# Weights stationary and both token tiles moving in the feed forward products, from the fourth chunk on

## The chip, the cores and the metric

The kernel runs on one core of a Trainium2 chip. The metric is the device time of one execution in microseconds, measured over several runs. Its input is one sequence of 256 tokens with 1,024 features, all in fp32, and the weights of three transformer layers, which lie in HBM.

## The reference

Three layers are computed one after the other on `x` of shape 256 x 1024. The first layer is a feed forward, a hybrid mixer (sparse attention and a gated recurrence) and a feed forward, with RMS norms ahead of each. The second and third layers have a feed forward, a mixer (forgetting attention, then latent attention "MLA"), a feed forward and a gate, each followed by a layer norm. The change is in the six feed forwards:

```python
def swiglu(x, w_gu, w_down):                    # layer 1, twice: D_FF = 2752
    gate, up = jnp.split(x @ w_gu, 2, axis=-1)
    return (jax.nn.silu(gate) * up) @ w_down
h = h + 0.5 * swiglu(rms_norm(h, ffn1_norm[l]), ffn1_w_gu[l], ffn1_w_down[l])
...
def swiglu_2(x, w_in, w_out):                   # layers 2 and 3, four times: D_FF_2 = 2816
    h = x @ w_in
    gate, up = h[..., :D_FF_2], h[..., D_FF_2:]
    return (jax.nn.silu(gate) * up) @ w_out
x = post_norm(x, 0.5 * swiglu_2(x, ffn1_w_in[i], ffn1_w_out[i]), ln_g[i, 0], ln_b[i, 0])
```

## The kernel before

The 256 tokens are two tiles of 128, `T` = 0 and 1. For each tile a Python generator (`net`) writes out the whole network, and `run` takes turns between the two: a step takes one unit of weights, and tile 1 follows `lag_at` units behind tile 0 (5, 3, 5 and 4 units in the feed forwards f1, f2, g1 and g2). The order that results is a static one; a scheduler may exchange instructions that wait for something, and gives priority to those written under `urgent`.

Every large product is done in three, since operands are split into a high and a low part (`mm3`, L348 to L350: high x high, high x low, low x high). They are of the type fp32r. The activations lie transposed in tiles `xh` and `xl` (a row block of 128 features by 128 tokens is the stationary operand), and the weights move, up to 512 columns at a time.

Weights come in units (`plan`, `ffn_units`), 512 KB for most, by SyncE's DMA queue into `wr` tiles of 128 x 512 (L312). ScalarE copies each to a high part (L319) and VectorE subtracts to get the low part (L320); both parts are `w` tiles, 42 in all, each 2,048 bytes wide. `AHEAD` = 2 units are written ahead of the one in use.

A feed forward (`ffn`, L580) goes through the hidden units in chunks of 256 (11 chunks; the last has 192 or 256). `up(c)` multiplies x by the gate and up columns of a chunk, 24 products of 512 columns for a token tile (eight row blocks times three), into one PSUM bank. ScalarE takes the tanh (L592) and VectorE forms silu(gate) x up (L593, L595 or L597). One unit into the next chunk's products, `turn` transposes the 128 x 256 result by two TensorE transposes (L358) into bank `tr`, and `split` (L353, L354) gives `hT` in two parts. `down(c-1)` then multiplies `hT` (stationary) by the down weights, 12 products of 512 columns for a chunk and token tile, into the two banks `a`, which collect over all chunks. `done` adds them to x (L572).

A token tile has four PSUM banks: `mm`, `tr` and twice `a`. Behind an RMS norm (f1, f2) the products take x without its factor 1/rms; the factor is a scalar per token, which is a partition there, and comes in by the tanh's scale and at L597.

In the MLA layer `mla_kv` (L1197) has another form: for token tile 0 it computes the keys of both tiles, with the weights stationary and 256 token columns of the tiles `ckh` and `ckl` moving:

```python
nc.tensor.matmul(o, wh[:, hs], xh, start=k == 0, stop=False)    # L1211
nc.tensor.matmul(o, wh[:, hs], xl, start=False, stop=False)     # L1212
nc.tensor.matmul(o, wl[:, hs], xh, start=False, stop=k == 1)    # L1213
```

Other products that the prediction uses: L870 (gated recurrence, plain fp32, 64 columns moving), L1294 (MLA values, plain fp32, 128 columns), L779 (compressed blocks, plain fp32, 256 columns; plain fp32 runs each product as two passes, each of them a record), and L1121 (forgetting gate, fp32r; the stationary operand is one column repeated 128 times, `fsel[:, h:h+1].to_broadcast([P, P])`).

Tiles are laid out in SBUF by `places`: `w`, `xh`, `xl`, `s2`, `wr`, `keep` and others, one behind the other, all with widths that are multiples of 512 bytes.

Of the kernel before, what the change touches and what calls it, by code (L numbers as in the profile page):

```python
# [12 lines left out]
FR = mybir.dt.float32r  # L13
U8 = mybir.dt.uint8
AF = mybir.ActivationFunctionType
# [12 lines left out]
LEVELS = [2, 4, 8, 16, 32, 64]  # L28

AHEAD = 2  # L30
N_WR = 6
N_S2 = 20
N_WARM = 6
N_W = 42
N_SE = 8
HP = 100
HALF = 512
# [17 lines left out]
L_M1 = 5  # L55


def ffn_units(tag, wg, wd, F, extra=()):
    nch = -(-F // 256)

    def up(c):
        f0 = 256 * c
        fw = min(256, F - f0)
        cols = [(f0, f0 + fw), (F + f0, F + f0 + fw)]
        return [(tag + "u", "s", [(wg, P * k, P * k + P, cols) for k in (2 * j, 2 * j + 1)])
                for j in range(4)]

    def down(c):
        f0 = 256 * c
        fw = min(256, F - f0)  # L70
        return [(tag + "d", "s", [(wd, f0 + r, min(f0 + r + P, F), [(0, D)])])
                for r in range(0, fw, P)]

    out = up(0)
    for c in range(1, nch):
        out += up(c) + (list(extra) if c == 3 else []) + down(c - 1)
    return out + down(nch - 1)


def col_units(tag, w, cols, K, per):  # L80
# [184 lines left out]
class Net:  # L265
    def __init__(self, nc, tc, sb, ps, a, units, offs):
        self.nc, self.tc, self.sb, self.ps, self.a = nc, tc, sb, ps, a
        self.units, self.offs = units, offs
        self.c = {}
        self.nw = 0  # L270
        self.live = deque()
        self.sh = {}
        self.uid = 0


# [81 lines left out]
        n = src.shape[0]  # L357
        self.nc.tensor.transpose(out, src, self.c["ident"][0:n, 0:n])  # L358

    def xt_tiles(self, n=8):  # L360
        hi = self.t("xh", [P, n, P], 4, FR)
        lo = self.t("xl", [P, n, P], 4, FR)
        return hi, lo

    @urgent
    def to_xT(self, halves, dst=None, k0=0):
        hi, lo = dst or self.xt_tiles()
# [113 lines left out]
    @urgent  # L481
    def scaled_xT(self, src, key, vs):
        nc = self.nc
        gb = self.gain(key)
        hs = [self.s2(), self.s2()]
        for j, h in enumerate(hs):
            cs = slice(512 * j, 512 * j + 512)
            nc.vector.tensor_tensor(h, src[:, cs], gb[:, cs], op=OP.mult)
        return self.to_xT(hs), self.scales(vs)

    def scales(self, vs):
        r = self.rstd(vs[0], 1e-6, extra=vs[1])
        sc = self.t("sc", [P, 8], 4)
        self.nc.vector.tensor_scalar(sc[:, 0:1], r, 0.5, None, op0=OP.mult)
        self.nc.vector.tensor_tensor(sc[:, 1:2], r, r, op=OP.mult)
        return sc

    def first_xT(self, x):
        xT = self.xt_tiles()
# [78 lines left out]


    def ffn(self, tag, xT, F, done, hook=None, sc=None):  # L580
        nc = self.nc
        nch = -(-F // 256)
        accs = []
        hts = {}

        def up(c):
            fw = min(256, F - 256 * c)
            pz = yield from self.dense(tag + "u", xT, 4, 2 * fw, mid=lambda: turn(c - 1),
                                       bank="mm" if c else "a")
            w = self.s2()  # L590
            t, h = w[:, 0:fw], w[:, 256:256 + fw]
            nc.scalar.activation(t, pz[:, 0:fw], AF.Tanh, scale=0.5 if sc is None else sc[:, 0:1])  # L592
            nc.vector.scalar_tensor_tensor(t, t, 1.0, pz[:, 0:fw], op0=OP.add, op1=OP.mult)  # L593
            if sc is None:
                nc.vector.tensor_tensor(h, t, pz[:, fw:2 * fw], op=OP.mult)  # L595
            else:
                nc.vector.scalar_tensor_tensor(h, t, sc[:, 1:2], pz[:, fw:2 * fw],  # L597
                                               op0=OP.mult, op1=OP.mult)
            hts[c] = (w, h, fw)

        def turn(c):
            if c < 0:
                return
            w, h, fw = hts[c]
            tp = self.pt("tr")
            rows = []
            for i, f in enumerate(range(0, fw, P)):
                n = min(P, fw - f)
                rows.append(n)
                self.tr(tp[0:n, P * i:P * i + P], h[:, f:f + n])  # L610
            hT = self.s2(dt=FR)
            if rows == [P, P]:
                self.split(hT[:, 0:256], hT[:, 256:512], tp[:, 0:256])
            else:
                for i, n in enumerate(rows):
                    self.split(hT[0:n, P * i:P * i + P], hT[0:n, 256 + P * i:256 + P * i + P],
                               tp[0:n, P * i:P * i + P])
            hts[c] = (hT, rows)

        def down(c):  # L620
            if c == 0:
                accs.extend((self.pt("a"), self.pt("a")))
            hT, rows = hts.pop(c)
            ws = []
            for i, n in enumerate(rows):
                (w,) = yield tag + "d"
                ws.append(w)
                if c < nch - 1:
                    part(c, hT, rows, i, w, (0, 1))
            if c == nch - 1:  # L630
                for j in range(2):
                    for i, w in enumerate(ws):
                        part(c, hT, rows, i, w, (j,))
                    done(j, accs[j])

        def part(c, hT, rows, i, w, js):
            n = rows[i]
            x = (hT[0:n, P * i:P * i + P], hT[0:n, 256 + P * i:256 + P * i + P])
            for j in js:
                self.mm3(accs[j], x, w[j], c == 0 and i == 0, c == nch - 1 and i == len(rows) - 1)  # L640
# [581 lines left out]
    def mla(self, T, xT, done):  # L1222
# [27 lines left out]
            nc.scalar.activation(r, tp, AF.Copy)  # L1250
            qr.append(r.rearrange("p (i t) -> p i t", i=4))

        oTs = [self.xt_tiles(), self.xt_tiles()]
        st = {}

        def proj_q(g):
# [103 lines left out]
    def net(self, T):  # L1360
        nc = self.nc

        def halves(w):
            return [w[:, 0:512], w[:, 512:1024]]
# [22 lines left out]
        st, res = self.residual(x, 0.25, "rms")  # L1387
        yield from self.ffn("f2", xT, F1, res, sc=sc)
        self.rms(x, self.gain("final_norm"), halves(x), vs=st["v"])
        for l in range(2):  # L1390
            xT = self.to_xT(halves(x))
# [11 lines left out]
            xT = self.to_xT(halves(x))  # L1403
# [78 lines left out]

def places(n):
    n.wt()
    n.T = 0
    n.xt_tiles()
    n.s2()
    n.t("wr", [P, HALF], N_WR)
    n.keep(P, 4)
# [76 lines left out]
```

## Time and profile before

| what | value |
|---|---|
| median of 3 runs | 1681.42 us (1681.36 to 1682.54) |
| the profiled execution | 1679.82 us |
| its span | 1678.0 us |
| mean granted TensorE clock | 0.998 |
| TensorE busy | 1649.1 us, 98% |
| VectorE, ScalarE busy | 1111.4 us (66%), 937.1 us (56%) |
| read from HBM | 290.29 MB, 174 GB/s over the span |

The span is the time from the first to the last instruction of the profiled execution; 1.8 us lie around it. PE is TensorE's matmul, PEld its weight load, DVE is VectorE, ACT ScalarE, POOL GpSimd and SP SyncE. A matmul's record runs from its start to the modelled end of its results, and the next one starts before that end; so the distance between starts, and not the duration, tells what a matmul takes of TensorE's time. The clock 1.00 stands for 2.4 GHz.

### The profile page before, as it was taken

The numbers are of one execution on the slowest core, as the hardware profiler recorded it, in microseconds if no ns is written. First come the engines' busy times: TensorE is split into PE (matmuls) and PEld (weight loads), VectorE is DVE, ScalarE is ACT, GpSimd is POOL, SyncE is SP. The second block draws the span as 40 slices with busy tenths as digits, with TensorE's granted clock in tenths as the row PEclk, the third lists the DMA queues.
The fourth block names the chain that finished last, engine by engine and source line by source line (L and its number), as shares of the span: only waits on it lengthen the run. The fifth ranks groups of instructions, "written<-read, shape, count | busy, mean of one in ns | idle before, by whom it ended". The sixth has DMA issues, their size and how long they took to land.

```text
span 1678.0 us, 24853 instructions
## 1 busy us (share of the span) xinstructions
PE 1649.1 (98%) x8020; PEld 1343.1 (80%) x8020; DVE 1111.4 (66%) x2309; ACT 937.1 (56%) x1899; POOL 23.8 (1%) x43
## 2 busy tenths in 40 slices
PE   9999999999999999999999999999999999999997
PEld 7888777778888788887888888778888888788886
DVE  7666666676666766677557666885666865766666
ACT  7555655555555555555555555555555775555553
POOL 0000000000000000000000000000000000000000
PEclk9999999999999999999999999999999999999999
DMA  8856544336655566655436565565665633566652
GB/s 280 273 179 176 176 166 126 101 120 195 188 188 178 174 189 189 187 164 164 145 107 213 188 188 188 179 217 168 195 189 163 210 99 100 184 206 189 188 176 76
DMA packets 160547, 293.00 MB, mean 175 GB/s; under 512 B 18208, under 2 KB 27168, under 8 KB 160416
## 3 DMA queue, kind: packets, MB, share of 16 engines
q1 hardware_dynamic: 160128, 291.34, 55.8%
q8 instruction: 63, 1.03, 0.2%
q14 instruction: 68, 0.56, 0.1%
q10 hardware_dynamic: 288, 0.07, 0.0%
HBM read 290.29 MB, written 1.05 MB: 174 GB/s over the span
## 4 chain that ended last, share of the span: by engine, by line
PE 87%; DVE 6%; DMA 3%; ACT 2%; issue 2%; POOL 1%; DVEq 0%; POOLq 0%; SPq 0%; ACTq 0%
PE mm L348 16%; PE mm L350 15%; PE mm L349 15%; PE a L348 10%; PE a L349 9%; PE a L350 9%; PE tr L358 4%; DMA wr<-wp 2%; DVE w L320 1%; DVE x L555 1%; PE a L779 1%; ACT w L319 1%; DVE x L560 1%; DVE x L572 1%; PE a L1294 1%
## 5 line engine op out<-in xcount | busy, mean ns | idle before, releaser
L320 DVE TENSOR_TENSOR w<-wr,w 128x512 fp32r<-128x512 f32 (+3 forms) x1058 | 703.6, 679 | 351.9 <-ACT w L319 165.2
L319 ACT ACTIVATE w<-wr 128x512 fp32r<-128x512 f32 (+3 forms) x1058 | 649.3, 623 | 396.6 <-PE mm L349 233.3
L348 PE MATMUL mm<-w,xh 128*128 128x512 f32 (+3 forms) x1200 | 477.4, 398 | 0.6 <-DVE s L597 0.5
L350 PE MATMUL mm<-w,xl 128*128 128x512 f32 (+3 forms) x1200 | 464.8, 387 | 0.0
L349 PE MATMUL mm<-w,xh 128*128 128x512 f32 (+3 forms) x1200 | 463.8, 387 | 0.0
L348 PEld LDWEIGHTS mm<-w,xh 128*128 128x128 f32 x1200 | 225.7, 188 | 44.6 <-issue 4.4
L350 PEld LDWEIGHTS mm<-w,xl 128*128 128x128 f32 x1200 | 225.5, 188 | 43.3
L349 PEld LDWEIGHTS mm<-w,xh 128*128 128x128 f32 x1200 | 226.2, 189 | 38.7 <-issue 0.6
L348 PE MATMUL a<-w,s 128*128 128x512 f32 x531 | 208.1, 392 | 0.5 <-ACT s L353 0.5
L349 PE MATMUL a<-w,s 128*128 128x512 f32 x531 | 207.4, 391 | 0.0
L350 PE MATMUL a<-w,s 128*128 128x512 f32 x531 | 207.2, 391 | 0.2 <-DVE s L354 0.2
L348 PEld LDWEIGHTS a<-w,s 128*128 128x128 f32 x531 | 99.6, 188 | 25.0 <-issue 3.6
L348 PE MATMUL a<-w,xh 128*128 128x512 f32 (+2 forms) x304 | 118.8, 392 | 0.8 <-ACT xh L353 0.7
L349 PE MATMUL a<-w,xh 128*128 128x512 f32 (+2 forms) x304 | 118.0, 389 | 0.8 <-DVE w L320 0.7
L350 PE MATMUL a<-w,xl 128*128 128x512 f32 (+2 forms) x304 | 116.7, 387 | 0.0
L350 PEld LDWEIGHTS a<-w,s 128*128 128x128 f32 x531 | 99.6, 188 | 21.1 <-DVE s L354 0.6
L349 PEld LDWEIGHTS a<-w,s 128*128 128x128 f32 x531 | 99.7, 188 | 19.9
L353 ACT ACTIVATE s<-tr 128x256 fp32r<-128x256 f32 (+2 forms) x137 | 50.6, 371 | 70.8 <-PE tr L358 70.7
L354 DVE TENSOR_TENSOR s<-tr,s 128x256 fp32r<-128x256 f32 (+2 forms) x137 | 56.5, 413 | 47.9 <-ACT s L353 47.7
L358 PE MATMUL tr<-const,s 128*128 128x128 f32 (+1 forms) x436 | 77.5, 274 | 3.9 <-DVE s L595 1.8
L358 PEld LDWEIGHTS tr<-const,s 128*128 128x128 f32 (+1 forms) x436 | 55.9, 140 | 29.7 <-DVE s L472 2.7
L348 PEld LDWEIGHTS a<-w,xh 128*128 128x128 f32 x304 | 57.1, 188 | 14.8 <-ACT xh L353 3.3
(280 smaller groups left out, 1355.0 us busy)
## 6 DMA issues: line engine op xcount, KB each, us to landing
wr<-wp SPq DMA_DIRECT2D x994, 256.0 KB, 2.7
gb<-vec SPq DMA_DIRECT2D x21, 512.0 KB, 4.3
wr<-wp SPq DMA_DIRECT2D x32, 192.0 KB, 2.4
w<-wp SPq DMA_DIRECT2D x16, 256.0 KB, 5.3
wr<-wp SPq DMA_DIRECT2D x16, 160.0 KB, 2.4
wr<-wp SPq DMA_DIRECT2D x8, 168.0 KB, 2.3
wr<-wp SPq DMA_DIRECT2D x8, 140.0 KB, 2.1
out<-x SPq DMA_DIRECT2D x4, 256.0 KB, 2.0
```

The lines of the kernel that those rows point to most:

```text
L319: nc.scalar.activation(hi[:, 0:w], r[:, 0:w], AF.Copy)
L320: nc.vector.tensor_tensor(lo[:, 0:w], r[:, 0:w], hi[:, 0:w].bitcast(FT), op=OP.subtract)
L348: mm(out, xh, wh, start=start, stop=False)
L349: mm(out, xh, wl, start=False, stop=False)
L350: mm(out, xl, wh, start=False, stop=stop)
L353: self.nc.scalar.activation(hi, src, AF.Copy)
L354: self.nc.vector.tensor_tensor(lo, src, hi.bitcast(FT), op=OP.subtract)
L358: self.nc.tensor.transpose(out, src, self.c["ident"][0:n, 0:n])
L555: nc.vector.scalar_tensor_tensor(y[:, cs], y[:, cs], nm, g[:, cs], op0=OP.add, op1=OP.mult)
L560: nc.vector.scalar_tensor_tensor(y[:, cs], y[:, cs], r, b[:, cs], op0=OP.mult, op1=OP.add)
L572: self.nc.vector.scalar_tensor_tensor(x[:, cs], acc, c, x[:, cs], op0=OP.mult, op1=OP.add, accum_out=s)
L779: nc.tensor.matmul(hp[0:2 * nb, 256 * kv:256 * kv + 256], kbs[kv][:, cc].rearrange("p g b -> p (g b)"), u[i][0], start=cc == 0, stop=cc == 15)
```

## The change

The feed forward's chunks become narrower: the first has 192 or 256 hidden units, the other 20 have 128. The first three (`APART`) are done as before, each token tile by itself. From the fourth on, `up_both` does both token tiles at once, in the program of tile 0: the weights are stationary, 128 gate columns and then 128 up columns, and the 256 token columns of x move. The result has hidden units in its partitions and tokens in its columns, as the down product wants it, so there is no transpose. Its accumulator is bank `mm` or `tr` of tile 0 by turns. Tile 1 takes the same units and writes no instruction for them.

For this `xh` and `xl` hold both token tiles side by side (`xt_pair`), in two buffers each that are 64 floats wider than needed, and x begins 48 floats (`FFN_AT`) into the tile. There are 41 `w` tiles in place of 42. In f1 and f2 the factor 1/rms is now needed along the columns: `spread` gets it by a product of a matrix of ones with a diagonal, and the last factor goes into the residual's scalar. `down(c)` comes four chunks (`HOLD`) after `up(c)`; before it was one. The last two chunks' down products are grouped by output half.

```diff
+HOLD = 4
+APART = 3
+FFN_AT = 48
-N_W = 42
+N_W = 41
+def ffn_chunks(F):
+    first = F - P * ((F - P - 1) // P)
+    return [(0, first)] + [(f, P) for f in range(first, F, P)]
 def ffn_units(tag, wg, wd, F, extra=()):
-    nch = -(-F // 256)
+    chunks = ffn_chunks(F)
+    nch = len(chunks)
...
-        return [(tag + "u", "s", [(wg, P * k, P * k + P, cols) for k in (2 * j, 2 * j + 1)])
-                for j in range(4)]
+        per = 2 if fw > P else 4
+        return [(tag + "u", "s", [(wg, P * k, P * k + P, cols) for k in range(j, j + per)])
+                for j in range(0, 8, per)]
...
-    out = up(0)
-    for c in range(1, nch):
-        out += up(c) + (list(extra) if c == 3 else []) + down(c - 1)
-    return out + down(nch - 1)
+    out = []
+    for c in range(nch):
+        out += up(c) + (list(extra) if c == 3 else []) + (down(c - HOLD) if c >= HOLD else [])
+    for c in range(nch - HOLD, nch):
+        out += down(c)
+    return out
...
-    def xt_tiles(self, n=8):
-        hi = self.t("xh", [P, n, P], 4, FR)
-        lo = self.t("xl", [P, n, P], 4, FR)
-        return hi, lo
+    def xt_pair(self, n, w, at=0):
+        return tuple(self.t(tag, [P, 2 * D + 64], 2, FR)[:, at:at + 2 * D].rearrange("p (n w) -> p n w", w=w)
+                     for tag in ("xh", "xl"))
+
+    def xt_tiles(self, at=0):
+        if self.T == 0:
+            self.xfull = self.xt_pair(8, S, at)
+            self.xfifo.append(self.xfull)
+            w = self.xfull
+        else:
+            w = self.xfifo.popleft()
+        return tuple(v[:, :, P * self.T:P * self.T + P] for v in w)
...
-        self.nc.vector.tensor_scalar(sc[:, 0:1], r, 0.5, None, op0=OP.mult)
-        self.nc.vector.tensor_tensor(sc[:, 1:2], r, r, op=OP.mult)
+        for i, f in enumerate((0.5, 1.0, 0.25)):
+            self.nc.vector.tensor_scalar(sc[:, i:i + 1], r, f, None, op0=OP.mult)
         return sc
+    def spread(self, r, out):
+        nc = self.nc
+        dg, one = self.t("se", [P, S], N_SE)[:, 0:P], self.t("se", [P, S], N_SE)[:, 0:P]
+        nc.gpsimd.memset(one, 1.0)
+        nc.vector.tensor_scalar(dg, self.c["ident"], r, None, op0=OP.mult)
+        tp = self.pt("tr")
+        nc.tensor.matmul(tp[:, 0:P], one, dg, start=True, stop=True)
+        nc.scalar.activation(out, tp[:, 0:P], AF.Copy)
...
+        def mid(c):
+            if c == 0:
+                if sc is not None:
+                    self.spread(sc[:, 1:2], pair["r"][:, P * T:P * T + P])
+                pair["spread", T] = True
+            elif c <= APART:
+                turn(c - 1)
...
+        def up_both(c):
+            if T == 1:
+                for i in range(2):
+                    yield tag + "u"
+                    if i == 0:
+                        mid(c)
+                return
+            xh, xl = pair["x"]
+            pz = self.pt("tr" if c % 2 else "mm")
+            mm = nc.tensor.matmul
+            k = 0
+            for i in range(2):
+                u = yield tag + "u"
+                if i == 1:
+                    mid(c)
+                for wh, wl in u:
+                    for j in range(2):
+                        o, ms = pz[:, S * j:S * j + S], slice(P * j, P * j + P)
+                        mm(o, wh[:, ms], xh[:, k, :], start=k == 0 and j == 0, stop=False)
+                        mm(o, wh[:, ms], xl[:, k, :], start=False, stop=False)
+                        mm(o, wl[:, ms], xh[:, k, :], start=False, stop=k == 7 and j == 1)
+                    k += 1
+            t = self.t("se", [P, S], N_SE)
+            gate = pz[:, 0:S]
+            if sc is not None:
+                g = self.t("se", [P, S], N_SE)
+                nc.vector.tensor_tensor(g, gate, pair["r"], op=OP.mult)
+                gate = g
+            nc.scalar.activation(t, gate, AF.Tanh, scale=0.5)
+            nc.vector.scalar_tensor_tensor(t, t, 1.0, gate, op0=OP.add, op1=OP.mult)
+            nc.vector.tensor_tensor(t, t, pz[:, S:2 * S], op=OP.mult)
+            hT = self.s2(dt=FR)
+            self.split(hT[:, 0:S], hT[:, S:2 * S], t)
+            pair[c] = hT
...
-        yield from up(0)
-        for c in range(1, nch):
-            yield from up(c)
+        first = [True]
+        for c in range(nch):
+            yield from (up if c < APART else up_both)(c)
             if c == 3 and hook:
                 yield from hook()
-            yield from down(c - 1)
-        turn(nch - 1)
-        yield from down(nch - 1)
+            if c >= HOLD:
+                yield from down([c - HOLD])
+        for c in range(nch - HOLD, nch - 2):
+            yield from down([c])
+        yield from down([nch - 2, nch - 1])
...
-        st, res = self.residual(x, 0.25, "rms")
+        st, res = self.residual(x, sc[:, 2:3], "rms")
```

## Rows read from the trace of the kernel before

**Rows 1.** The page, busy us of each engine, share of the span, instructions.

```profile
PE 1649.1 (98%) x8020; PEld 1343.1 (80%) x8020; DVE 1111.4 (66%) x2309; ACT 937.1 (56%) x1899; POOL 23.8 (1%) x43
```

**Rows 2.** Windows: busy PE, PEld, DVE, ACT, POOL; granted clock; DMA share; GB/s.

```profile
580.00:740.00 160.00, 160.00 (x725) 131.88 (x724) 98.93 (x176) 85.27 (x156) 0.00 (x0) 1.00 0.61 188
900.00:1060.00 160.00, 160.00 (x725) 131.84 (x724) 100.90 (x176) 86.07 (x156) 0.00 (x0) 1.00 0.61 193
```

**Rows 3.** Who waited for whom: us in all, times, longest.

```profile
ACT w L319 <- PE mm L349: 233.3, 188, 3.5
...
PE tr L358 <- DVE x L560: 4.5, 11, 0.9
```

**Rows 4.** Timeline of TensorE in a feed forward: start us, us, what, count.

```profile
910.45 0.39 PE L350 MATMUL mm<-w,xl 128*128 128x512 f32 x1
910.69 0.38 PE L358 MATMUL tr<-const,s 128*128 128x128 f32 x2
...
911.14 0.39 PE L349 MATMUL mm<-w,xh 128*128 128x512 f32 x1
...
912.97 0.39 PE L348 MATMUL mm<-w,xh 128*128 128x512 f32 x1
...
915.01 0.39 PE L348 MATMUL a<-w,s 128*128 128x512 f32 x1
```

**Rows 5.** Timeline of TensorE, MLA keys: first and last of 23 products.

```profile
1295.25 0.28 PE L1211 MATMUL mm<-keep,w 128*128 128x256 f32 x1
...
1297.88 0.28 PE L1212 MATMUL a<-keep,w 128*128 128x256 f32 x1
```

**Rows 6.** Timeline of TensorE, merged series of other products, and one alone.

```profile
245.69 2.78 PE L779 MATMUL a<-w,s 128*30 128x256 f32 x12
...
248.81 0.72 PE L870 MATMUL a<-s,s 128*128 128x64 f32 x5
...
786.39 0.28 PE L1121 MATMUL a<-keep,misc 128*128 128x256 f32 x1
...
786.39 0.63 PE L1121 MATMUL a<-keep,misc 128*128 128x256 f32 x4
...
1386.85 1.06 PE L1294 MATMUL a<-pT,s 128*128 128x128 f32 x8
```

**Rows 7.** Groups by form, TensorE: busy us, mean ns of one, idle before.

```profile
L779 PE MATMUL a<-w,s 128*30 128x256 f32 x64 | 16.0, 383 | 0.0
L1294 PE MATMUL a<-pT,s 128*128 128x128 f32 x96 | 13.8, 279 | 0.1
L870 PE MATMUL a<-s,s 128*128 128x64 f32 x96 | 12.7, 275 | 0.1
```

**Rows 8.** Timeline of TensorE, one transpose between products.

```profile
770.30 0.39 PE L350 MATMUL mm<-w,xl 128*128 128x512 f32 x1
770.53 0.27 PE L358 MATMUL tr<-const,se 128*128 128x128 f32 x1
...
770.87 0.39 PE L349 MATMUL mm<-w,xh 128*128 128x512 f32 x1
```

**Rows 9.** Groups of VectorE and of ScalarE: busy us, mean ns, idle before.

```profile
L320 DVE TENSOR_TENSOR w<-wr,w 128x512 fp32r<-128x512 f32 (+3 forms) x1058 | 703.6, 679 | 351.9 <-ACT w L319 165.2 <-PE mm L349 148.7 <-PE a L349 26.1
L354 DVE TENSOR_TENSOR s<-tr,s 128x256 fp32r<-128x256 f32 (+2 forms) x137 | 56.5, 413 | 47.9 <-ACT s L353 47.7
L593 DVE SCALAR_TENSOR_TENSOR s<-s,mm 128x256 f32<-128x256 f32 (+1 forms) x120 | 49.6, 414 | 21.1 <-ACT s L592 20.8
L595 DVE TENSOR_TENSOR s<-s,mm 128x256 f32<-128x256 f32 x80 | 33.6, 420 | 2.5
...
L319 ACT ACTIVATE w<-wr 128x512 fp32r<-128x512 f32 (+3 forms) x1058 | 649.3, 623 | 396.6 <-PE mm L349 233.3 <-PE a L349 98.2 <-DMA wr<-wp 17.7
L353 ACT ACTIVATE s<-tr 128x256 fp32r<-128x256 f32 (+2 forms) x137 | 50.6, 371 | 70.8 <-PE tr L358 70.7
L592 ACT ACTIVATE s<-mm 128x256 f32<-128x256 f32 x80 | 30.0, 375 | 29.6 <-PE mm L350 29.6
```

More of the change, by code (lines that the diff above doesn't have):

```diff
@@ L55 @@
 L_M1 = 5
+def ffn_chunks(F):
+    first = F - P * ((F - P - 1) // P)
+    return [(0, first)] + [(f, P) for f in range(first, F, P)]
 def ffn_units(tag, wg, wd, F, extra=()):
-    nch = -(-F // 256)
+    chunks = ffn_chunks(F)
+    nch = len(chunks)
     def up(c):
-        f0 = 256 * c
-        fw = min(256, F - f0)
+        f0, fw = chunks[c]
         cols = [(f0, f0 + fw), (F + f0, F + f0 + fw)]
-        return [(tag + "u", "s", [(wg, P * k, P * k + P, cols) for k in (2 * j, 2 * j + 1)])
-                for j in range(4)]
+        per = 2 if fw > P else 4
+        return [(tag + "u", "s", [(wg, P * k, P * k + P, cols) for k in range(j, j + per)])
+                for j in range(0, 8, per)]
     def down(c):
-        f0 = 256 * c
-        fw = min(256, F - f0)
-        return [(tag + "d", "s", [(wd, f0 + r, min(f0 + r + P, F), [(0, D)])])
+        f0, fw = chunks[c]
+        return [(tag + "d", "s", [(wd, f0 + r, min(f0 + r + P, f0 + fw), [(0, D)])])
                 for r in range(0, fw, P)]
-    out = up(0)
-    for c in range(1, nch):
-        out += up(c) + (list(extra) if c == 3 else []) + down(c - 1)
-    return out + down(nch - 1)
+    out = []
[4 more added lines that the diff above has]
+    return out
 def col_units(tag, w, cols, K, per):
@@ L272, in __init__ @@
         self.sh = {}
+        self.xfifo = deque()
         self.uid = 0
@@ L358, in tr, with to_xT @@
         self.nc.tensor.transpose(out, src, self.c["ident"][0:n, 0:n])
-    def xt_tiles(self, n=8):
-        hi = self.t("xh", [P, n, P], 4, FR)
-        lo = self.t("xl", [P, n, P], 4, FR)
-        return hi, lo
+    def xt_pair(self, n, w, at=0):
[9 more added lines that the diff above has]
+        return tuple(v[:, :, P * self.T:P * self.T + P] for v in w)
     @urgent
-    def to_xT(self, halves, dst=None, k0=0):
-        hi, lo = dst or self.xt_tiles()
+    def to_xT(self, halves, dst=None, k0=0, at=0):
+        hi, lo = dst or self.xt_tiles(at)
         for j, h in enumerate(halves):
@@ L488, in scaled_xT @@
             nc.vector.tensor_tensor(h, src[:, cs], gb[:, cs], op=OP.mult)
-        return self.to_xT(hs), self.scales(vs)
+        return self.to_xT(hs, at=FFN_AT), self.scales(vs)
     def scales(self, vs):
@@ L493, in scales @@
         sc = self.t("sc", [P, 8], 4)
-        self.nc.vector.tensor_scalar(sc[:, 0:1], r, 0.5, None, op0=OP.mult)
-        self.nc.vector.tensor_tensor(sc[:, 1:2], r, r, op=OP.mult)
-        return sc
+        for i, f in enumerate((0.5, 1.0, 0.25)):
+            self.nc.vector.tensor_scalar(sc[:, i:i + 1], r, f, None, op0=OP.mult)
+        return sc
+    def spread(self, r, out):
[6 more added lines that the diff above has]
+        nc.scalar.activation(out, tp[:, 0:P], AF.Copy)
     def first_xT(self, x):
-        xT = self.xt_tiles()
+        xT = self.xt_tiles(FFN_AT)
         with self.tc.high_priority(offset=HP):
@@ L580, in ffn @@
     def ffn(self, tag, xT, F, done, hook=None, sc=None):
-        nc = self.nc
-        nch = -(-F // 256)
+        nc, T = self.nc, self.T
+        chunks = ffn_chunks(F)
+        nch = len(chunks)
         accs = []
         hts = {}
+        if T == 0:
+            self.pair = {"x": self.xfull}
+            if sc is not None:
+                self.pair["r"] = self.t("se", [P, S], N_SE)
+        pair = self.pair
+        pair["in", T] = True
+        def mid(c):
[5 more added lines that the diff above has]
+                turn(c - 1)
         def up(c):
-            fw = min(256, F - 256 * c)
-            pz = yield from self.dense(tag + "u", xT, 4, 2 * fw, mid=lambda: turn(c - 1),
+            fw = chunks[c][1]
+            pz = yield from self.dense(tag + "u", xT, 4 if fw > P else 2, 2 * fw, mid=lambda: mid(c),
                                        bank="mm" if c else "a")
@@ L601, in turn @@
         def turn(c):
-            if c < 0:
-                return
             w, h, fw = hts[c]
@@ L617, in turn @@
                                tp[0:n, P * i:P * i + P])
-            hts[c] = (hT, rows)
-        def down(c):
-            if c == 0:
-                accs.extend((self.pt("a"), self.pt("a")))
[L623 to L630, printed above, removed]
+            hts[c] = [(hT[0:n, P * i:P * i + P], hT[0:n, 256 + P * i:256 + P * i + P])
+                      for i, n in enumerate(rows)]
@@ new lines, in up_both @@
+        def up_both(c):
[11 more added lines that the diff above has]
+                u = yield tag + "u"
+                assert pair["in", 1]
+                if i == 1:
[7 more added lines that the diff above has]
+                    k += 1
+            assert pair["spread", 1]
+            t = self.t("se", [P, S], N_SE)
+            gate = pz[:, 0:S]
+            if sc is not None:
+                g = self.t("se", [P, S], N_SE)
[7 more added lines that the diff above has]
+            pair[c] = hT
@@ new lines, in hidden, with down @@
+        def hidden(c):
+            if c < APART:
+                return hts.pop(c)
+            hT = pair.pop(c) if T else pair[c]
+            return [(hT[:, P * T:P * T + P], hT[:, S + P * T:S + P * T + P])]
+        def down(cs):
+            if cs[0] == 0:
+                accs.extend((self.pt("a"), self.pt("a")))
+            todo = []
+            for c in cs:
+                for x in hidden(c):
+                    (w,) = yield tag + "d"
+                    if len(cs) > 1:
+                        todo.append((x, w))
+                        continue
+                    for j in range(2):
+                        self.mm3(accs[j], x, w[j], first[0], False)
+                    first[0] = False
+            if todo:
@@ L631, in down @@
                 for j in range(2):
-                    for i, w in enumerate(ws):
-                        part(c, hT, rows, i, w, (j,))
+                    for i, (x, w) in enumerate(todo):
+                        self.mm3(accs[j], x, w[j], False, i == len(todo) - 1)
                     done(j, accs[j])
[L636 to L640, printed above, removed]
@@ L1251, in proj_qr @@
             qr.append(r.rearrange("p (i t) -> p i t", i=4))
-        oTs = [self.xt_tiles(), self.xt_tiles()]
+        oh, ol = self.xt_pair(16, P)
+        oTs = [(oh[:, k:k + 8, :], ol[:, k:k + 8, :]) for k in (0, 8)]
         st = {}
@@ L1386, in net @@
         pre("final_norm")
-        st, res = self.residual(x, 0.25, "rms")
+        st, res = self.residual(x, sc[:, 2:3], "rms")
         yield from self.ffn("f2", xT, F1, res, sc=sc)
@@ L1390, in net @@
         for l in range(2):
-            xT = self.to_xT(halves(x))
+            xT = self.to_xT(halves(x), at=FFN_AT)
             pre(("g", l, 0), ("b", l, 0))
@@ L1402, in net @@
             self.layer_norm(x, st, ("g", l, 1), ("b", l, 1))
-            xT = self.to_xT(halves(x))
+            xT = self.to_xT(halves(x), at=FFN_AT)
             pre(("g", l, 2), ("b", l, 2))
@@ L1484, in places @@
     n.wt()
-    n.T = 0
-    n.xt_tiles()
+    n.xt_pair(8, S)
     n.s2()
```

## The prediction

> **What bounds the kernel now.** I read the page's busy shares first. TensorE is busy 98% of the span, VectorE 66% and ScalarE 56% [rows 1]. A busy TensorE may still be waiting, so next come the windows inside the feed forward stretches: TensorE fills each whole window at a granted clock of 1.00 (the 2.4 GHz level), while VectorE is busy 62 to 63% of it and ScalarE 53 to 54% [rows 2]. The waits settle which side leads: ScalarE, which splits the loaded weights, waits 233 us in all for a product to free a weight tile, and TensorE's longest own wait is 4.5 us in all [rows 3]. So weights are always early and the kernel lasts as long as the sum of TensorE's steps. What counts is the distance from one product's start to the next; the listed durations of about 0.39 us overlap and don't add up.
>
> Two distances carry the argument. Nine products of 512 columns take 912.97 to 915.01, 0.2267 us each [rows 4]. A product that keeps weights stationary and moves 256 columns is already in the kernel, in the MLA keys: 22 steps from 1295.25 to 1297.88, 0.1195 us each [rows 5]. Columns alone need 512/2.4 = 213.3 ns and 256/2.4 = 106.7 ns. Both forms cost 13 ns more than that, once per product and not per column.
>
> **The change, part by part.** *Products.* Only the first chunk of a feed forward keeps its width. In each of the six, ten chunks of 256 hidden units times 48 products go (three split products, eight row blocks, two token tiles), so 2,880 of 512 columns, 2880 x 0.2267 = 652.9 us. In their place come 20 chunks of 128 times 48, so 5,760 of 256 columns (the two narrow chunks still done per token tile also move 256). The columns are the same and the 13 ns are paid twice as often, unless the price of one falls. At 0.1195 it is 688.3 us, a loss of 35.4.
>
> What can that price be? The code before gives every tile a width that is a multiple of 512 bytes, and operands begin at multiples of 128 floats, so moving and stationary operand always begin at the same place modulo 512. After the change the moving x begins 48 floats (192 bytes) into a tile of 8,448 bytes, so 64 bytes before a multiple of 256. No row shows that relation, so I bound it. Below: a weight load of 128 columns at every step sets a floor. In a series, the first start to the last is the merged length less one duration. Eight passes that move 128 columns stand (1.06 - 0.279)/7 = 0.1116 us apart, and five that move only 64 columns (0.72 - 0.275)/4 = 0.111 [rows 6, 7]. Half the columns save nothing, so the load sets that step; 5760 x 0.1116 = 642.8, a gain of 10.1. Above: 0.1195, as the aligned rows have it. Two rows say what the 13 ns hang on. Single passes of plain fp32 over 256 columns stand (2.78 - 0.383)/11 = 0.218 us apart [rows 6, 7], with a load beside each; these stream at half the rate and pay only 5 ns over 213. And the forget gate's products, which move 256 fp32r columns but read a stationary operand that is one column repeated, stand (0.63 - 0.28)/3 = 0.117 us apart [rows 6]. So the extra depends on where the load reads while the moving side streams at full rate; it is not a constant of the product. Changing where they read relative to each other can therefore change it. At 0.117 the products cost 673.9, a loss of 21.0. I take 0.114, halfway from the repeated column to the floor: 656.6 us, +3.7. The repeated column is the nearest row in which the two reads don't run through equal offsets; a proper shift should do at least as well as it, and cannot pass the floor.
>
> A rule speaks against this step. The Trainium skill, page "TensorE: Matmul & The Clock Gate", section "Step-by-step: what each phase is for", says the array has two read ports into SBUF, and that "Loading the next tile's weights doesn't steal SBUF read bandwidth from the running matmul". By that rule the shift does nothing and the aligned price stays. The trace bears it out only in part, since the price did move with the load's addresses, 0.1195 against 0.117 us; no run here shows a shifted operand.
>
> *Transposes.* Before, each chunk and token tile has two transposes in the middle of the next up product. From the product ahead of them at 910.45 to the second one behind them at 911.14 is 0.69 us, of which two products are 0.45: a pair costs 0.23 us [rows 4]. One transpose alone costs 770.87 - 770.30 - 0.45 = 0.12 [rows 8]. Eleven chunks, two tiles, six times are 132 pairs, 30.4 us. After, weights stationary gives the hidden units already transposed: 12 pairs (the wide first chunk) and 24 single ones are left, 2.8 + 2.8 us. Gain 24.8 us, all on TensorE's chain.
>
> *Spread.* The two feed forwards behind an RMS norm need 1/rms along the columns, since tokens now lie there. That is one plain fp32 product of 128 columns per token tile, two passes at about 0.11 and the switch, four times: +1.0 us. Its memset, diagonal and copy come in the first chunk, three chunks ahead of use.
>
> *ScalarE and VectorE.* One chain now serves both tiles at 256 columns where one served a tile at 256 before: tanh 0.37 us, two VectorE steps of 0.41 to 0.42, a split of 0.37 and 0.41 [rows 9]. Per 16 us there are two of each, as before; 36 gate multiplications (some 0.42 us each) are new. They lie beside 16 us of products, with VectorE free for 37%: nothing. If that cover were gone they would be 15 us.
>
> *Weights.* A unit stays 512 KB and two tiles each of high and low parts, in DMAs, splits and queue order; 41 instead of 42 tiles hardly matter, as up weights come free without waiting for the second token tile. A down unit may now be used up in 1.4 us, less than the 2.7 us from unit to unit before. ScalarE and VectorE need 1.3 to 1.4 us for a unit (two tiles of 0.62 and 0.68 [rows 9]), and the tiles hold several units ahead: nothing, or up to 1 us at the end of each feed forward.
>
> *Waits.* Down four chunks later means the last hidden chunk has three chunks' down products between it and its use. The new wait is one of a PSUM bank. In the first shared chunk the accumulator of the first token tile sits in the bank that the third chunk's transpose needs; that transpose and the split behind it must follow the shared chunk's tanh and two VectorE steps, 0.37 + 0.41 + 0.42 = 1.2 us. If TensorE meets it directly it stands 1.3 us, six times 7.8; the next chunk's products use the other bank and can go first, then it is nothing. I take 2 us.
>
> *Sum.* +3.7 - 24.8 + 1.0 + 2.0 = -18.1 us. The profiled execution took 1679.8 us, 1678.0 of it span; it becomes 1661.7. The median of the runs is 1.6 above the profiled one, so 1663.
>
> **Rivals.** *The shift does nothing* (0.20): products stay at 0.1195, +35.4 instead of +3.7. The time is 1695, up to 1701 with the bank wait in full. For it: the aligned rows, and the page's rule. Against: the repeated column. It decides from a price of 0.1177 up, where the sum passes +0.2%.
>
> *Half an effect* (0.12): the price is that of the repeated column, 0.117. The sum is 21.0 - 24.8 + 3.0, so 1681, no change. For it: it is the only measured price with different addresses. Against: even there the reads meet in some columns.
>
> *The load alone sets the step* (0.08): 0.1116 and the bank wait is covered, -10.1 - 24.8 + 1.0 = -33.9, so 1648. For it: between loads 0.1116 is very steady. Against: with 256 columns moving, both streams are almost equally long, and neither then has slack.
>
> **How the numbers follow.** The forecast case (prices from 0.112 to 0.116, 1652 to 1675) has 0.60. My likeliest time is 1663. The range must take in the load's floor and the aligned price: 1648 to 1698, which leaves out about 1 in 10. Faster by over 0.2% (about what a measurement of this kernel can tell from no change) are the forecast, the load's floor and none of the rest: 0.68. The half effect gives most of no change and a little of slower: 0.10 and 0.02; with the first rival slower is 0.22.
>
> **What would show it.** Steps of the shared up products near 0.114 us; near 0.12 the first rival is right. About 96 fewer pairs of transposes and 24 single ones. Loads busy for much more of a feed forward window than now. TensorE's idle before the third chunk's transpose under 1 us. The prediction fails if the shifted price lies at either end, if products meet weights that were not split in time, or if the bank wait recurs.

## The result, and the profile after

The change made the kernel slower: 1692.12 us median (1691.74 to 1692.34) against 1681.39 beside it. The ratio on record is 1.0068 [1.0053, 1.0083] (the bracket is its 95% interval; the two medians alone give 1.0064). That is inside the predicted range and on the wrong side of its forecast. The profiled execution took 1692.18 us, 12.4 more than that of before; the terms below are held against these 12.4.

The page after, busy us of each engine, share of the span and instructions:

```profile
PE 1651.6 (98%) x10692; PEld 1466.6 (87%) x10692; DVE 1126.3 (67%) x2389; ACT 935.7 (55%) x1927; POOL 25.0 (1%) x47
```

The same windows as [rows 2], after:

```profile
580.00:740.00 160.00, 159.95 (x1154) 150.76 (x1153) 99.46 (x182) 84.25 (x160) 0.41 (x2) 1.00 0.64 188
900.00:1060.00 160.00, 160.00 (x1144) 150.65 (x1143) 104.44 (x183) 88.21 (x162) 0.00 (x0) 0.99 0.64 192
```

Against [rows 1, 2], loads are busy 151 us of 160 instead of 132, and TensorE still fills the windows with ScalarE and VectorE far from full. So the work beside TensorE stayed hidden, as forecast, and what counts is again the distance between TensorE's starts.

**The price of a product.** The timeline of TensorE after: the first and last of 48 shared products, and the product behind them.

```profile
634.24 0.28 PE L681 MATMUL mm<-xh,w 128*128 128x256 f32 x1
...
639.78 0.28 PE L683 MATMUL mm<-xh,w 128*128 128x256 f32 x1
639.90 0.39 PE L359 MATMUL a<-w,s 128*128 128x512 f32 x1
```

5.54 us for 47 steps is 0.1179 us; other such series of the steady stream come to the same within 0.0001. I use 0.1178. The forecast had 0.114; the aligned row had 0.1195 [rows 5].

Not every series runs at that price. The second and the last product of the third shared chunk of the first feed forward, after:

```profile
49.95 0.28 PE L682 MATMUL tr<-xl,w 128*128 128x256 f32 x1
...
55.16 0.28 PE L683 MATMUL tr<-xh,w 128*128 128x256 f32 x1
```

5.21 us for 46 steps is 0.1133 us, with x at the same place in its tile. Such series stand only near the starts of feed forwards, about 5% of the shared steps; behind them the stream settles at 0.1178. What sets the two apart isn't shown.

What a whole stretch of 256 hidden units costs comes out of the timeline as a period: before, from one pair of transposes to the same pair of the next chunk; after, from the first product of one shared chunk to that of the second one behind it. Before:

```profile
637.03 0.38 PE L358 MATMUL tr<-const,s 128*128 128x128 f32 x2
...
653.85 0.38 PE L358 MATMUL tr<-const,s 128*128 128x128 f32 x2
```

After:

```profile
625.87 0.28 PE L681 MATMUL tr<-xh,w 128*128 128x256 f32 x1
...
642.62 0.28 PE L681 MATMUL tr<-xh,w 128*128 128x256 f32 x1
```

16.82 us became 16.75. Both hold the same 24 down products; 48 wide products and two pairs of transposes have become 96 narrow products. The prediction's prices give 48 x 0.2267 + 0.46 - 96 x 0.114 = 0.40 us won per period; 0.07 was won. Over the 54 periods (5,184 shared products, 96 to a period) that is 18 us missing.

**A new stop.** TensorE's own waits after, us in all, times, longest:

```profile
PE tr L369 <- DVE x L588: 11.6, 11, 4.9
PE tr L369 <- DVE x L491: 2.7, 2, 2.2
PE tr L369 <- DVE se L694: 2.1, 1, 2.1
```

The first of these answers to the 4.5 us, at most 0.9 at a time, in [rows 3]. The timeline shows where the long ones lie: TensorE at the start of a feed forward, after.

```profile
575.14 0.28 PE L361 MATMUL mm<-w,xl 128*128 128x256 f32 x1
577.57 0.70 PE L369 MATMUL tr<-const,x 128*128 128x128 f32 x4 [2.15 <-DVE x L491]
...
898.80 1.07 PE L369 MATMUL tr<-const,x 128*128 128x128 f32 x4 [2.04 <-DVE x L588]
...
1123.93 0.92 PE L369 MATMUL tr<-const,x 128*128 128x128 f32 x4 [4.90 <-DVE x L588]
...
1471.21 0.66 PE L369 MATMUL tr<-const,x 128*128 128x128 f32 x4 [1.98 <-DVE x L588]
```

VectorE beside the first of them:

```profile
576.76 1.42 DVE L491 SCALAR_TENSOR_TENSOR x<-x,col,gb 128x512 f32<-128x512 f32 x2 [0.18 <-POOL col L474]
578.09 0.28 DVE L636 SCALAR_TENSOR_TENSOR s<-s,mm 128x128 f32<-128x128 f32 x1
578.41 0.29 DVE L638 TENSOR_TENSOR s<-s,mm 128x128 f32<-128x128 f32 x1
```

Token tile 0 has begun the feed forward; token tile 1's norm is still on VectorE (576.76). Tile 0 has finished chunk 1, and chunk 2 writes the bank `mm` as well, which stays occupied until VectorE has read chunk 1 out at 578.09 and 578.41, behind the norm. So nothing of tile 0 can be next in TensorE's order, and it stands until tile 1's x is there to transpose. The banks are named as they were before. But before, chunk 1 was 24 products of 512 columns, 24 x 0.2267 = 5.4 us; now it is 24 of 256, 2.8 us.

The same four places in windows (the third figure from the end is the granted clock), each behind the stop:

```profile
578.05:581.46 3.41, 3.41 (x13) 2.86 (x12) 2.59 (x6) 1.30 (x3) 0.00 (x0) 0.50 0.47 162
581.46:590.00 8.54, 8.54 (x61) 7.86 (x60) 4.84 (x9) 4.76 (x9) 0.00 (x0) 1.00 0.58 171
...
898.90:902.31 3.41, 3.41 (x14) 2.98 (x15) 2.61 (x6) 1.19 (x2) 0.00 (x0) 0.50 0.72 233
1124.18:1127.59 3.41, 3.41 (x13) 2.61 (x12) 2.62 (x6) 1.52 (x3) 0.00 (x0) 0.50 0.64 211
1472.34:1475.75 3.41, 3.41 (x11) 2.73 (x10) 1.98 (x3) 1.39 (x3) 0.00 (x0) 0.50 0.49 175
```

Having stood, TensorE runs 3.41 us at 0.50, the 1.2 GHz level. The stops sum to 2.15 + 2.04 + 4.90 + 1.98 = 11.1 us; four stretches at half clock cost at most 4 x 1.7 = 6.8. The kernel before had stops of its own, among them this one ahead of a transpose in a feed forward, which the change no longer has:

```profile
PE tr L358 <- DVE s L595: 1.8, 1, 1.8
```

So by the two pages TensorE's idle time (the span less its busy time) rose from 28.9 to 38.8 us, by 9.9 and not by all of the new stops.

### The profile page after: what moved, and what is told of

It is laid out like the page before. It is cut to its first block, busy times and chain, and to the rows that moved or that the text cites. A ratio compares the mean times of both kernels' runs of the same rounds, so it can differ in the third digit from the quotient of the medians.

```text
span 1690.4 us, 30248 instructions
## 1 busy us (share of the span) xinstructions
PE 1651.6 (98%) x10692; PEld 1466.6 (87%) x10692; DVE 1126.3 (67%) x2389; ACT 935.7 (55%) x1927; POOL 25.0 (1%) x47
## 4 chain that ended last, share of the span: by engine, by line
PE 87%; DVE 5%; ACT 2%; DMA 2%; issue 2%; POOL 1%; DVEq 0%; SPq 0%; POOLq 0%; ACTq 0%
PE a L359 10%; PE a L361 10%; PE a L360 10%; PE mm L681 6%; PE mm L683 6%; PE mm L682 6%; PE tr L681 6%; PE tr L683 6%; PE tr L682 6%; PE mm L359 4%; PE mm L361 4%; PE mm L360 4%; PE tr L369 3%; DMA wr<-wp 2%; DVE w L331 1%
## 5 line engine op out<-in xcount | busy, mean ns | idle before, releaser
L681 PE MATMUL mm<-xh,w 128*128 128x256 f32 x864 | 243.3, 282 | 0.0
L682 PE MATMUL mm<-xl,w 128*128 128x256 f32 x864 | 243.0, 281 | 0.0
L681 PE MATMUL tr<-xh,w 128*128 128x256 f32 x864 | 242.9, 281 | 0.0
L683 PE MATMUL mm<-xh,w 128*128 128x256 f32 x864 | 242.9, 281 | 0.0
L682 PE MATMUL tr<-xl,w 128*128 128x256 f32 x864 | 242.4, 281 | 0.0
L683 PE MATMUL tr<-xh,w 128*128 128x256 f32 x864 | 242.4, 281 | 0.0
L359 PE MATMUL a<-w,s 128*128 128x512 f32 (+1 forms) x531 | 207.6, 391 | 0.0
L361 PE MATMUL a<-w,s 128*128 128x512 f32 (+1 forms) x531 | 207.1, 390 | 0.0
L360 PE MATMUL a<-w,s 128*128 128x512 f32 (+1 forms) x531 | 207.0, 390 | 0.0
L681 PEld LDWEIGHTS mm<-xh,w 128*128 128x128 f32 x864 | 162.7, 188 | 3.3 <-issue 0.4
L683 PEld LDWEIGHTS mm<-xh,w 128*128 128x128 f32 x864 | 165.4, 191 | 0.0
L681 PEld LDWEIGHTS tr<-xh,w 128*128 128x128 f32 x864 | 162.4, 188 | 3.4 <-ACT s L364 0.4
L683 PEld LDWEIGHTS tr<-xh,w 128*128 128x128 f32 x864 | 165.3, 191 | 0.0
L682 PEld LDWEIGHTS mm<-xl,w 128*128 128x128 f32 x864 | 162.4, 188 | 2.5
L682 PEld LDWEIGHTS tr<-xl,w 128*128 128x128 f32 x864 | 162.2, 188 | 2.5
L359 PE MATMUL mm<-w,xh 128*128 128x512 f32 (+4 forms) x432 | 148.9, 345 | 0.6 <-DVE s L640 0.6
```

What stands on the lines that cost most here:

```text
L359: mm(out, xh, wh, start=start, stop=False)
L360: mm(out, xh, wl, start=False, stop=False)
L361: mm(out, xl, wh, start=False, stop=stop)
L681: mm(o, wh[:, ms], xh[:, k, :], start=k == 0 and j == 0, stop=False)
L682: mm(o, wh[:, ms], xl[:, k, :], start=False, stop=False)
L683: mm(o, wl[:, ms], xh[:, k, :], start=False, stop=k == 7 and j == 1)
```

## The experiments

Two theories stood against each other for the missing time. **Price:** the shift of the operands is worth less than assumed, so the products took back the transposes' gain. **Start:** the stops at the feed forwards' starts are the loss, and the price is nearly right. A third, **lag**, put the stops on the distance of the two token tiles and not on the bank. Each chip ran the kernel before as well; its medians were 1678.93, 1681.31 and 1681.01 us, so only ratios compare across chips.

### e1_at0 and e4_at32: the operands' place

```diff
-FFN_AT = 48
+FFN_AT = 0      # e4_at32: 32
```

> x begins at the start of its tile (0 in place of 48 floats), so both operands of a shared up product begin at the same place modulo 512 bytes; nothing else changes. Theory 1 (the shift is worth a little): a shared up product goes from the 117.5 ns read in the changed kernel to the 119.5 of the aligned key products, 5760 x 2 ns = 11.5 us slower than the changed kernel, so near 1704 us. Rival (the place does nothing, and 117.5 is what the form costs in this stretch): within 2 us of the changed kernel's 1692. If the alignment is worth as much as my prediction had it (5 ns), 1719.

> x begins 32 floats (128 bytes) into its tile. Theory 1 with a smooth effect of the place: a shared up product between 117.5 and 119.5 ns, so 1692 to 1704 us. Rival (any place off the 512 byte grid is as good as any other): 117.5 ns and 1692.

e1_at0 took 1708.78 us (before 1678.93), 1.0175 [1.0157, 1.0193]; e4_at32, a single run, 1707.43 (ratio of the medians 1.0170). Their series of 48 products, TensorE's timeline, e1_at0:

```profile
632.38 0.28 PE L681 MATMUL tr<-xh,w 128*128 128x256 f32 x1
...
638.01 0.28 PE L683 MATMUL tr<-xh,w 128*128 128x256 f32 x1
```

and e4_at32:

```profile
631.10 0.28 PE L681 MATMUL tr<-xh,w 128*128 128x256 f32 x1
...
636.74 0.29 PE L683 MATMUL tr<-xh,w 128*128 128x256 f32 x1
```

5.63/47 = 0.1198 and 5.64/47 = 0.1200 us: with nothing or 32 floats the aligned price is back. In e1_at0 the third shared chunk of the first feed forward has it too (46 steps from 50.85 to 56.37 us, 0.1200), where the change had 0.1133. So the shift does work, and in the steady stream it is worth 2 ns of a step, not 5.5. Over 5,760 products 2.0 ns is 11.5 us; the 1.07% between the two ratios is 18 us, by their intervals 14 to 22. The two spans, 1706.1 and 1690.4 us, lie 15.7 apart. By the sums of TensorE's steps in the two traces 12.9 of these are the products of 256 columns, and 3.5 are the down products, which took longer as well although their own operands did not move; why is not shown. The stops got 0.7 shorter. e4_at32 fits neither of its two expectations: 32 floats don't lie between the two prices, they do nothing.

### e2_bank: chunk 1 in another bank

```diff
-    bank="mm" if c else "a")
+    bank="mm" if c > 1 else "a")
```

> The second chunk's accumulator goes to the free second buffer of bank a, so the third chunk's products need not wait until the second chunk's tanh and multiplications have emptied bank mm. Theory 2 (at the start of a feed forward token tile 0 runs out of products because chunk 3 waits for that bank, and TensorE then stands before token tile 1's transposes): five stalls of 2.1 to 5.1 us, 11.7 us in all, shrink to under 1 us each, and the four stretches of 3.4 us at half clock behind them go; together 12 to 18 us, so 1674 to 1680 us. Rival (TensorE stands because of the order in which token tile 1's transposes are placed, whatever bank is free): the stalls stay, 1690 to 1693.

1678.89 us (before 1678.93), 0.9997 [0.9985, 1.001]. The timeline of TensorE at the same start, e2_bank:

```profile
575.71 0.28 PE L361 MATMUL a<-w,xl 128*128 128x256 f32 x1
575.83 0.28 PE L359 MATMUL mm<-w,xh 128*128 128x256 f32 x1
...
578.07 0.28 PE L360 MATMUL mm<-w,xh 128*128 128x256 f32 x1
578.18 0.62 PE L369 MATMUL tr<-const,x 128*128 128x128 f32 x4
```

and the window around it, and the waits:

```profile
574.50:590.00 15.50, 15.50 (x109) 14.24 (x108) 13.01 (x26) 10.44 (x22) 0.55 (x1) 1.00 0.72 223
```

```profile
PE tr L369 <- DVE x L588: 5.5, 11, 2.1
PE tr L369 <- DVE s L491: 1.6, 3, 0.6
PE tr L369 <- DVE se L694: 2.7, 1, 2.7
```

With chunk 1 in bank `a`, 20 products of chunk 2 run from 575.83 to 578.07, where TensorE had stood, and the clock stays at 1.00. Three of the four stops are gone, and the one of 4.90 us is left with 2.1. One line takes back 0.71% of the time, 11.9 us. So the stops hang on the bank (e8_lag3 below shows that they hang on the lag as well). But the kernel is then only as fast as before: with the start mended, the price alone has taken the gain. Both theories are true in part.

### e3_wide and e5_banks: other ways to give tile 0 work

e3_wide makes the first two chunks wide and all separate chunks use bank `a`; e5_banks keeps the chunks and only orders the banks.

```diff
 e3_wide
-APART = 3
+APART = 2
-    return [(0, first)] + [(f, P) for f in range(first, F, P)]
+    return [(0, first), (first, 2 * P)] + [(f, P) for f in range(first + 2 * P, F, P)]
 e3_wide and e5_banks
-    bank="mm" if c else "a")
+    bank="a")
 e5_banks
-            pz = self.pt("tr" if c % 2 else "mm")
+            pz = self.pt("mm" if c % 2 else "tr")
```

> The first two chunks are wide (192 or 256, then 256 hidden units) and done for each token tile by itself, both in bank a, then 18 shared chunks of 128. Token tile 0 has as many products ahead of the first shared chunk as it had before (48 instead of 48 in two narrow and one wide chunk, but in two free banks). Theory 2: the stalls at the start go as with the bank alone, and 576 products of 256 columns become 288 of 512 (576 x 117.5 ns - 288 x 227 ns = 2.3 us less), the 24 single transposes become 12 pairs (no change): 1671 to 1678 us. Rival (the runway is not the cause): 1688 to 1692.

> All three separate chunks collect in bank a, and the shared chunks take bank mm first and tr second (they took tr first), so the third chunk's transpose finds tr free. Bank theory: the stall of 2.8 us before that transpose in the first feed forward goes, and the third chunk has a free bank as well: 2 to 4 us less than with the second chunk's bank alone, a ratio to the kernel before of 0.9975 to 0.9985. Rival (that stall comes from the first feed forward's other work on ScalarE and VectorE, not from the bank): ratio 0.9995 to 1.0000.

e3_wide: 1679.72 us (1678.93), 1.0002 [0.9989, 1.0014]. That is as fast as e2_bank and above the 1671 to 1678 expected; its trace has a stop of 3.2 us (behind L640) in the first feed forward. e5_banks: 1678.07 us (1681.31), 0.9984 [0.9972, 0.9995], the only version below before by more than its interval. TensorE's waits in e5_banks:

```profile
PE tr L369 <- DVE x L588: 5.2, 11, 1.8
PE tr L369 <- DVE s L640: 2.4, 2, 1.8
```

The stops at the starts are as short as in e2_bank. The wait of the forecast, at the third chunk's transpose for the first shared chunk's bank, is gone (L694 is not in the list), but a like one for L640 stands in its place with 1.8 us. Whether e5_banks is better than e2_bank, 0.9984 against 0.9997, lies within their intervals.

### m1_col and m2_mov: what the price consists of

Both stand on e2_bank; the shared up products keep their number, columns and loads, and only addresses change: m1_col loads one weight column 128 times, m2_mov moves one token's column 256 times.

```diff
 m1_col
+    vh, vl = (v[:, P * j:P * j + 1].to_broadcast([P, P]) for v in (wh, wl))
...        # vh, vl in place of wh[:, ms], wl[:, ms]
 m2_mov
+    vh, vl = (v[:, k, 0:1].to_broadcast([P, S]) for v in (xh, xl))
...        # vh, vl in place of xh[:, k, :], xl[:, k, :]
```

> As the kernel with the second chunk in bank a, but the shared up products load one weight column repeated 128 times in place of 128 columns, so the weight load reads one address; the gate and up values are left out of the computation. If what a shared product pays over its 106.7 ns of columns hangs on the load's reads (my prediction's view): 111.7 to 114 ns in place of 117.5, and 5184 x 4 ns = 21 us less, near 1658. If the repeated column is no better than a shifted operand, as the forget gate's rows suggest (117 ns): 1677 to 1679.

> As the kernel with the second chunk in bank a, but the shared up products move one token column repeated 256 times, so the moving side reads one address; the hidden values are left out of the computation. If the extra comes from the moving side's and the load's reads meeting: 111.7 to 114 ns a product and near 1658 us. If it is a fixed cost of an fp32r product: 117.5 ns and 1677 to 1679.

A single run each: 1663.95 and 1653.45 us (before 1681.31). TensorE's timeline, m1_col:

```profile
618.30 0.28 PE L682 MATMUL tr<-xh,w 128*128 128x256 f32 x1
...
623.64 0.28 PE L684 MATMUL tr<-xh,w 128*128 128x256 f32 x1
```

m2_mov:

```profile
615.27 0.27 PE L682 MATMUL tr<-xh,w 128*128 128x256 f32 x1
...
620.51 0.28 PE L684 MATMUL tr<-xh,w 128*128 128x256 f32 x1
```

5.34/47 = 0.1136 and 5.24/47 = 0.1115 us. With the moving side on one address the step falls to the spacing of bare loads, 0.1116 [rows 6]; with the load on one column it stops 2 ns above. So the floor of the prediction was right, and what lies above it depends on where the two sides read: 6.3 ns of the 117.8 go when the moving addresses no longer vary. That the two reads meet in parts of the memory fits this, but only addresses (and with them the values) were changed, not conflicts counted.

The Trainium skill, page "TensorE: Matmul & The Clock Gate", section "Step-by-step: what each phase is for", has loads not stealing read bandwidth from a running product. By that the three kernels should step alike; they step at 0.1178, 0.1136 and 0.1115, and the measurement decides.

### e6_at16: another place off the grid

e2_bank with `FFN_AT = 16` instead of 48.

> As the kernel with the second chunk in bank a, but x begins 16 floats (64 bytes) into its tile, on the other side of the grid. If only the distance of 64 bytes counts: 117.5 ns a product, 1677 to 1679 us. If the side counts (the moving side runs twice as fast as the load, so it should lead or trail): 119 to 120 ns and 1687 to 1692.

A single run: 1681.86 us (before 1681.31); 48 products from 623.74 to 629.28 us, 0.1179 us a step. 16 floats do what 48 do, 0 and 32 do nothing: of the four places tried, none gives more than 2 ns in the steady stream.

### e7_hold2: down two chunks later instead of four

e2_bank with `HOLD = 2` instead of 4.

> As the kernel with the second chunk in bank a, but the down products come two chunks after the up products in place of four. Theory (four chunks of distance are more than the hidden values need: their chain is some 2.4 us long and a shared chunk 5.6 us): no difference, a ratio of 0.999 to 1.001 to the kernel before. Rival (the distance hides the chain at the end of a feed forward, where no up products follow): six ends of 1 to 3 us each, ratio 1.003 to 1.010.

1683.74 us (1681.01), 1.0024 [1.0012, 1.0036], against e2_bank's 0.9997: between the two expectations. The step is unchanged: 629.71 to 635.25 us, 0.1179. The late down products are worth about 0.27%; its waits, the longest 0.9 us at L491 and 2.0 at L694, don't name a single place where the shorter hold loses.

### e8_lag3 and e9_banks_lag3: the distance of the token tiles

The change with a shorter lag in two stages, and e5_banks with the same.

```diff
-L_G1 = 5
-L_G2 = 4
+L_G1 = 3
+L_G2 = 3
```

> The changed kernel with its banks as they are, but token tile 1 follows 3 units behind in all of layer 2's and 3's feed forwards (it was 5 in the first and 4 in the second of each). Rival to the bank theory (the stalls at the start come from token tile 1 being too far behind, so that its layer norm ends late; the second feed forward of layer 1 has a lag of 3 and no such stall): stalls of 2.1 to 5.1 us shrink by 1 to 2 units of 1.36 us, half of the loss goes, ratio 1.001 to 1.004. Bank theory alone: the layer norm of token tile 1 comes earlier but token tile 0 still has no products for it to lie beside; less than 3 us of gain, ratio 1.005 to 1.007.

> Both: the banks (all separate chunks in a, shared chunks mm first) and the lag of 3. If bank and lag act on the same stalls: 2 us are left to gain at the start of layer 3's first feed forward, ratio 0.9970 to 0.9985. Rival (a shorter lag leaves token tile 0's end of each feed forward less covered): 0.9985 to 1.001.

e8_lag3: 1684.78 us (1681.01), 1.0018 [1.0005, 1.0031]. e9_banks_lag3: 1682.55 (1681.01), 1.0017 [1.0004, 1.003]. TensorE in e8_lag3 at the start that stood 2.15 us in the change, and behind the gate of the second layer:

```profile
576.91 0.66 PE L369 MATMUL tr<-const,x 128*128 128x128 f32 x4 [0.24 <-DVE x L491]
...
1104.27 0.39 PE L361 MATMUL mm<-w,s 128*128 128x512 f32 x1
1108.64 1.11 PE L369 MATMUL tr<-const,x 128*128 128x128 f32 x4 [3.98 <-DVE x L588]
```

Lag was right as well: with the tiles nearer, tile 1's x is there in time without any change of banks. But the stop of 4.90 us moved to tile 0's own norm, 3.98 us ahead of the feed forward. Of the 0.68% of loss 0.5 comes back. With the better banks the short lag only costs: 1.0017 against 0.9984, above either expectation; where it loses was not traced.

## Why the prediction failed

The likeliest case was 1663, faster; it came out at 1692. Held against the profiled execution's own difference:

| step | predicted | by the rows |
|---|---|---|
| products | +3.7 | 5760 x 0.1178 - 652.9 = +25.6 |
| transposes | -24.8 | -24.8: 428 of the group became 212, as the counts said; their price was not measured again |
| spread | +1.0 | not measured apart, +1.0 kept |
| bank wait, third chunk | +2.0 | +2.1, once, in the first feed forward |
| stops at four starts | none | +11.1 |
| half clock behind them | none | at most +6.8 |
| sum | -18.1 | +21.8; the difference of the spans and what lies around them is +12.4 |

Of the 9.4 us that the rows put too much, 3.3 are stops that the kernel before had as well, in these places or others (TensorE's idle time rose by 9.9, not by the 13.2 of the two rows), 2.5 are down products that got shorter (the sums of their steps in either trace, stops left out), and 2.2 are periods before of 16.82 us where the prices give 16.78. The rest isn't placed; the 6.8 at half clock is an upper bound.

**Where it failed, first:** "I take 0.114", and the reason for it, "a proper shift should do at least as well as" the repeated column "and cannot pass the floor". The second half held (m2_mov reaches 0.1115 and no steady stream passes it). The first did not: in the steady stream the shift does worse than a repeated column, 0.1178 against 0.1136 for the same products, and only some series near the starts reached 0.1133. The mechanism, a price that hangs on addresses, was right, and the term's size wrong. 0.114 lay halfway between two rows of other operations, with no row of a shifted operand. One of the two was weak: 0.117 comes from three steps, and times printed to 0.01 us leave (0.63 - 0.28)/3 anywhere from 0.113 to 0.120, so it did not show that the load's addresses matter; m1_col did, with 47 steps. The outcome of the rival "half an effect", 0.117 and no change, is what e2_bank showed, at 0.9997. The measured 0.1178 lies beyond the prediction's own break-even, (652.9 + 24.8 - 3.0)/5760 = 0.1171, and just past the 0.1177 from which it calls the kernel slower.

**Second:** the part on waits looked for banks at the third chunk's transpose alone. That wait came as sized, but once, and another order of the banks (e5_banks) left 1.8 of it. The one that cost was of another bank, at the start: two narrow separate chunks in a row use `mm`, and the step "the two narrow chunks still done per token tile also move 256" counted their columns and not the time they used to cover. By e2_bank this is 11.9 us of ratio, about the whole loss. Without it, the forecast would have been off by the price alone.

**Right:** the count of the transposes; ScalarE and VectorE at nothing (TensorE fills its windows); weights at nothing; the floor that the loads set; that the shift does something, against the first rival.

## What to carry to other kernels

When a chunk is made narrower, list what each engine runs while another tile's slow step is due, and check that consecutive chunks don't share a bank whose reader is queued behind that step. Where the forecast rests on a price that no row shows, work out the break-even first; if it lies within the bounds, as 0.1171 did between 0.1116 and 0.1195, measure that price by itself, with one operand's address held still, before the kernel is rebuilt around it. And mend the new wait before judging the idea: here one bank name was worth 0.7%.

## What the runs showed of the hardware

The step of a 256-column product with a load beside it changed, in a steady stream, with nothing but the operands' addresses: 0.1198 us at 0 and 0.1200 at 32 floats into the tile, 0.1178 at 48 and 0.1179 at 16, 0.1136 with one column loaded, 0.1115 with one column moved. The place alone does not fix it: at 48 floats one chunk ran at 0.1133 and the next ones at 0.1178, in one kernel. At 0 floats that chunk ran at 0.1200.

Stops of about 2 us did not always cost the clock. In the change the four above were followed by 0.50; the one of 2.08 us in the first feed forward, and one of 2.10 us in e2_bank, were not. TensorE and the clock behind these two, after and then e2_bank:

```profile
42.40:46.00 3.60, 3.60 (x31) 3.60 (x32) 3.60 (x10) 2.67 (x8) 0.00 (x0) 1.00 0.88 291
```

```profile
1117.40:1121.00 3.60, 3.57 (x19) 2.73 (x20) 3.37 (x10) 2.28 (x6) 0.00 (x0) 1.00 0.64 215
```

What tells them apart was not tried. The Trainium skill, page "TensorE: Matmul & The Clock Gate", section "What's actually happening", has the activity counted on a schedule that runs by itself and doesn't start with the kernel, by which a like stop could fall differently; no run here shows it.
